# All elementwise products and sums of tiles on VectorE instead of GpSimd

## The chip, the cores and the metric

The kernel runs on one core of a Trainium2 chip. A core has five engines that run their own instruction streams side by side: TensorE (matrix products; PE in the profile, with the loading of its weights shown apart as PEld), VectorE (DVE), ScalarE (ACT), GpSimd (POOL) and SyncE (SP), which here issues all the transfers between the chip's memory (HBM) and the core's memory (SBUF). Matrix products land in a small memory of their own, PSUM. Instructions of different engines wait for each other by semaphores; within one engine they run in the order in which they were issued.

The metric is the time of one execution on the device in microseconds (us), and of several executions the median.

## The reference, cut to what matters

The program is a stack of four layers over 2048 tokens of width 1024, all in 32-bit floating point, with a batch of one. Each layer has the same frame, and its own mixing inside:

```python
h   = x @ w_in                      # 1024 -> 2560 to 4360 columns
mix = ...                           # the layer's own mixing of h, width 1024
out = mix @ w_out                   # 1024 -> 1024
x   = layer_norm(alpha * x + out)   # layers 1 to 3
x   = x + out                       # layer 4, whose input is normed by rms_norm
```

The mixings: layer 1, a gated linear recurrence (chunked) beside sliding-window attention with rotary positions; layer 2, gated linear attention beside a spatial gating unit with a norm of its own; layer 3, retention with rotary positions beside a pooling over 2, 4, 8 and 16 tokens; layer 4, banded attention, a matrix memory with gates (mLSTM) and a depthwise convolution of width 31 with a norm. Nearly every part ends in a gate, such as

```python
o = o * silu(hg)                    # layer 1; the same form in layers 2 to 4
```

so elementwise products of tiles are everywhere, and that is what the change is about.

## The kernel before, in words

**Tiling.** The 2048 tokens are cut into four blocks of 512. A stage is one layer on one block. `run` goes through them in the order: layers 1, 2, 3, 4 for blocks 0 and 1 (layer 1 block 0, layer 1 block 1, layer 2 block 0, and so on), then the same for blocks 2 and 3: 16 stages. In a stage the 512 tokens are either four row tiles of 128 tokens (tokens on the partitions), or column tiles of 128 features by 512 tokens.

**Products in three parts.** Full precision of the large products is reached by splitting each operand in a high and a low part: `ah` and `al` for the activations, `hi` and `lo` (both in one buffer `whl`) for the weights, and three matmuls each, hi x hi, lo x hi and hi x lo. `weight` (from L439) loads a weight tile into `wst` (two buffers), casts it on ScalarE to the high part (L450) and subtracts on VectorE for the low part (L315 by way of `tt`). The pair is written to HBM (`wdr`, L454) and from the second block on it is only loaded (L446). `whl` has four buffers. So the first stage of each layer converts all its weights, and the other three load them.

**One stage.** `load_x` loads the transposed rows that the layer before has stored and splits them into `ah` and `al`. Then come the input projections: `in_b` and `in_b4` (features on the partitions; `in_b4` uses four weight tiles twice, for 256 tokens each), and `in_a` (tokens on the partitions). Between them stands the layer's mixing, whose result is kept in `mix`. Its parts are transposed and split again (`split_mix`, or `split_ch` where they are already in column tiles), and `out_proj` forms the output in two halves of 512 columns. It adds the residual (`big<-big,acc` in the profile), takes the mean and variance (`bn_stats`, `rstd1`), and norms. For the odd row tiles two VectorE instructions per half norm and scale at once (`big<-big,mv,u` and `big<-big,vy,u`). For the even row tiles ScalarE norms and the scaling is left to `tail`. The single-column instructions of `rstd1` are named `ve`, `vy`, `vh`, `vf` and `vt`; they form an inverse square root step by step, each from the one before.

**The tails.** `tail` (from L650) belongs to a finished stage, but is traced in the input projections of the next one: `out_proj` puts four calls in a list, and `in_b4` takes one after each of its first groups (`flush`). It transposes a row tile for the next layer, stores the transposed tile (`chn`, L670) and, for the even row tiles, scales and shifts the row tile in place with `lng` and `lnb` (two halves, a product and a sum each), then stores the row tile for the residual of the next layer (`rows`, L676). These stores, and the loads of weights, are all in SP's queue.

**What sets the order.** The kernel does not write out the order of instructions of an engine. A planner (the tile framework's scheduler) goes through the traced instructions with a model of their durations and issues on each engine what is ready and comes first by priority. Priority is the order of tracing, except in `with self.hp():`, which moves instructions 2500 places ahead (weights and gates are traced so), and `self.later(2000)`, which moves them back (the 62 instructions of the wide convolution). The framework also sets the waits.

**What runs on GpSimd before the change.** All of it by `tt` (from L314) with an engine given. In every stage of layers 1 to 3 `tail`; in `gate_mix` and in layer 1 the gates (`mix<-mix,g`, `mix<-mix,u`); in `split_ch` and layer 4 the low parts of channels of `mix` (`al<-mix,ah`); in layer 2 the scale and shift of the spatial unit's norm and its gate; in layer 3 two of three steps of the rotation and the first step of the pooling; in layer 4 a scaling before the convolution, the scale and shift of the norm behind it, the squares and the scaling of the head norm, the division in `ml_head` and two gates. Beside these GpSimd has only memsets, selects and four copies.

## Time and profile before

| | |
|---|---|
| median of 3 runs | 3770.92 us |
| lowest and highest | 3770.17 and 3778.20 us |
| the profiled execution, its own time | 3774.09 us |
| its span in the profile | 3772.3 us |
| mean granted clock of TensorE | 0.995 |
| TensorE busy | 97% |
| VectorE busy | 58% |
| ScalarE busy | 37% |
| GpSimd busy | 14% |

How to read the rows: a group gives line, engine, operation, output<-inputs by the program's names, shapes and the count, then its busy time in us and the mean of one in ns, then the idle time of the engine just before them and what ended it. A row of the waits gives who waited for whom, the total in us, how often, and the longest. A row of the timeline begins with the start in us and the length; where the engine stood idle before it, the idle time and its releaser stand in brackets. A row of the windows gives the stretch and its length, the busy time and count of PE, PEld, DVE, ACT and POOL, then TensorE's granted clock (1.00 is full speed), the share of the transfer engines in use and GB/s. Most vector operations have line 315, 312 or 321, the lines of the helpers `tt`, `stt` and `ts`, so that the names of the tiles tell them apart. Recorded durations of two VectorE instructions in a row can overlap by some 0.1 us.

### The profile page before, as it was taken

Reading aid. Unit: us, or ns where it says so; the run is one execution under the profiler, and the core shown is the slowest. Engines: PE = TensorE matmul, PEld = TensorE weight load, DVE = VectorE, ACT = ScalarE, POOL = GpSimd, SP = SyncE. Lnnn points to the kernel's source line nnn. Section 1 sums busy time; section 2 is a strip of 40 time slices with the busy share of each in tenths; the row PEclk is TensorE's granted clock in tenths of the full one; section 3 lists DMA queues with packets and bytes.
Section 4 is the critical chain, followed back from the end, with each engine's and each line's share of the span. In section 5 each row is a group of like instructions: output and inputs, shape, how many; then the busy total and the mean of one; then the engine's idle time right before and its main releaser. Section 6 shows DMA issues by size and latency. Waiting matters only on the chain.

```text
span 3772.3 us, 53592 instructions
## 1 busy us (share of the span) xinstructions
PE 3677.3 (97%) x20576; PEld 3100.4 (82%) x20576; DVE 2177.9 (58%) x5387; ACT 1384.2 (37%) x2889; POOL 542.1 (14%) x445
## 2 busy tenths in 40 slices
PE   7999999999999999999999999999999999999999
PEld 6788888887888888788888878888887878888887
DVE  6765556555655598577456455443544545872873
ACT  5636343323241354325254263312221313441441
POOL 0020111112121200300200201111121311011002
PEclk9999999999999999999999999999999999999999
DMA  6775567855886576752544645747565756435434
GB/s 229 261 263 177 187 239 273 311 199 195 300 304 215 213 260 223 261 197 101 208 179 164 226 152 187 255 161 256 185 231 206 253 193 246 146 140 209 177 123 157
DMA packets 161680, 798.04 MB, mean 212 GB/s; under 512 B 17936, under 2 KB 18064, under 8 KB 93840
## 3 DMA queue, kind: packets, MB, share of 16 engines
q1 hardware_dynamic: 161424, 794.62, 58.4%
q8 instruction: 162, 2.65, 0.3%
q14 instruction: 94, 0.77, 0.1%
HBM read 593.02 MB, written 201.52 MB: 211 GB/s over the span
## 4 chain that ended last, share of the span: by engine, by line
PE 49%; DVE 6%; DMA 2%; ACT 2%; issue 1%; POOL 0%; SPq 0%; DVEq 0%; POOLq 0%; ACTq 0%
PE acc L324 41%; PE mm L324 6%; PE mm L327 3%; DVE u L312 2%; DMA whl<-wdr 1%; DVE t L315 1%; ACT t L301 0%; DVE big L312 0%; DMA wst<-in_wo_dram 0%; DVE t L1034 0%; DVE ss L1400 0%; ACT u L301 0%; POOL mix L315 0%; DVE mix L312 0%; ACT u L1424 0%
## 5 line engine op out<-in xcount | busy, mean ns | idle before, releaser
L324 PE MATMUL acc<-whl,ah 128*128 128x512 f32 (+3 forms) x6144 | 1816.2, 380 | 15.1 <-DVE whl L315 4.1
L324 PEld LDWEIGHTS acc<-whl,ah 128*128 128x128 f32 x6144 | 1112.0, 188 | 242.9 <-issue 7.1
L324 PE MATMUL acc<-whl,al 128*128 128x512 f32 (+3 forms) x3072 | 1156.8, 377 | 0.0
L324 PE MATMUL acc<-ah,whl 128*128 128x256 f32 (+1 forms) x4096 | 1076.8, 346 | 46.0 <-DVE whl L315 17.3
L324 PEld LDWEIGHTS acc<-ah,whl 128*128 128x128 f32 x4096 | 707.1, 191 | 135.0 <-DVE whl L315 18.6
L324 PE MATMUL acc<-al,whl 128*128 128x512 f32 (+1 forms) x2048 | 699.2, 342 | 0.5 <-DVE al L315 0.2
L324 PEld LDWEIGHTS acc<-whl,al 128*128 128x128 f32 x3072 | 578.0, 188 | 114.0
L324 PEld LDWEIGHTS acc<-al,whl 128*128 128x128 f32 x2048 | 391.5, 191 | 40.5 <-issue 2.9
L315 DVE TENSOR_TENSOR whl<-wst,whl 128x1024 fp32r<-128x1024 f32 (+2 forms) x140 | 173.3, 1244 | 142.0 <-ACT whl L450 131.5
L315 POOL TENSOR_TENSOR big<-big,u 128x512 f32<-128x512 f32 x96 | 139.1, 1471 | 562.0 <-PE mm L327 421.6
L450 ACT CAST whl<-wst 128x1024 fp32r<-128x1024 f32 (+2 forms) x140 | 143.3, 1027 | 149.3 <-DMA wst<-in_wi_dram 76.1
L548 ACT CAST ah<-u 128x512 fp32r<-128x512 f32 x128 | 79.3, 619 | 307.0 <-PE acc L324 200.1
L312 DVE SCALAR_TENSOR_TENSOR g<-g,acc 128x512 f32<-128x512 f32 x80 | 54.6, 686 | 204.3 <-ACT g L301 204.2
L312 DVE SCALAR_TENSOR_TENSOR u<-mix,hdw,u 128x512 f32<-128x512 f32 x240 | 165.6, 742 | 0.1
L315 POOL TENSOR_TENSOR mix<-mix,g 128x512 f32<-128x512 f32 x56 | 77.4, 1385 | 592.2 <-DVE g L312 574.2
L312 DVE SCALAR_TENSOR_TENSOR big<-big,acc 128x512 f32<-128x512 f32 x128 | 86.7, 684 | 120.2 <-PE acc L324 118.5
L301 ACT ACTIVATE g<-acc 128x512 f32<-128x512 f32 x72 | 42.6, 596 | 232.0 <-PE acc L324 226.4
L301 ACT ACTIVATE t<-mm,cols 128x128 f32<-128x128 f32 (+2 forms) x272 | 99.6, 463 | 66.6 <-PE mm L327 62.7
L315 POOL TENSOR_TENSOR u<-u,lc 128x512 f32<-128x512 f32 (+1 forms) x64 | 68.0, 1070 | 326.1 <-issue 170.0
L315 DVE TENSOR_TENSOR al<-u,ah 128x512 fp32r<-128x512 f32 x128 | 89.7, 702 | 42.1 <-ACT ah L548 41.0
L324 PE MATMUL mm<-big,u 128*128 128x256 f32 (+2 forms) x616 | 94.3, 289 | 7.3 <-ACT big L923 1.8
L324 PEld LDWEIGHTS mm<-big,u 128*128 128x128 f32 x616 | 84.3, 191 | 16.0 <-ACT u L1424 3.2
(342 smaller groups left out, 4376.8 us busy)
## 6 DMA issues: line engine op xcount, KB each, us to landing
whl<-wdr SPq DMA_DIRECT2D x396, 1024.0 KB, 4.8
wdr<-whl SPq DMA_DIRECT2D x132, 1024.0 KB, 5.3
wst<-in_wi_dram SPq DMA_DIRECT2D x100, 512.0 KB, 6.9
rows<-big SPq DMA_DIRECT2D x48, 512.0 KB, 4.0
chn<-t SPq DMA_DIRECT2D x96, 256.0 KB, 6.3
u<-chn SPq DMA_DIRECT2D x96, 256.0 KB, 6.6
big<-rows SPq DMA_DIRECT2D x48, 512.0 KB, 7.1
wst<-in_wo_dram SPq DMA_DIRECT2D x32, 512.0 KB, 6.0
```

The costliest lines, as they stand in the source:

```text
L301: return self.nc.scalar.activation(out, in_, f, bias=bias, scale=scale)
L312: return self.nc.vector.scalar_tensor_tensor(out, in0, s, in1, op0, op1)
L315: return (eng or self.nc.vector).tensor_tensor(out, a, b, op)
L324: return self.nc.tensor.matmul(out, lhsT, rhs, start=start, stop=stop)
L327: return self.nc.tensor.transpose(out, in_, self.ident)
L450: nc.scalar.copy(hi, st)
L548: nc.scalar.copy(h, c4(st))
```

## The change

Everywhere `tt` was given GpSimd as its engine, the argument is dropped, so VectorE runs the instruction. The instructions, their operands and their order in the program stay the same; memsets, selects and copies stay on GpSimd. The planner orders the engines' streams anew from the changed program.

```diff
 def split_ch(self, p, k):
-        self.tt(self.al[:, p], m, self.ah[:, p].bitcast(F32), ALU.subtract, self.nc.gpsimd)
+        self.tt(self.al[:, p], m, self.ah[:, p].bitcast(F32), ALU.subtract)
...
 def tail(...):
-                self.tt(xi, xi, lng[i], ALU.mult, nc.gpsimd)
-                self.tt(xi, xi, lnb[i], ALU.add, nc.gpsimd)
+                self.tt(xi, xi, lng[i], ALU.mult)
+                self.tt(xi, xi, lnb[i], ALU.add)
...
 def gate_mix(...):
-            self.tt(m, m, g, ALU.mult, self.nc.gpsimd)
+            self.tt(m, m, g, ALU.mult)
...
 def layer2(...):
-            self.tt(s, s, sg, ALU.mult, nc.gpsimd)
-            self.tt(s, s, sb, ALU.add, nc.gpsimd)
+            self.tt(s, s, sg, ALU.mult)
+            self.tt(s, s, sb, ALU.add)
...
-            self.tt(us[t], us[t], g, ALU.mult, nc.gpsimd)
+            self.tt(us[t], us[t], g, ALU.mult)
...
 def layer3(...):
-            self.tt(sh, sh, S, ALU.mult, nc.gpsimd)
-            self.tt(s, s, sh, ALU.add, nc.gpsimd)
+            self.tt(sh, sh, S, ALU.mult)
+            self.tt(s, s, sh, ALU.add)
...
-                self.tt(cur[:, start:528], prev[:, start:528], prev[:, start - d:528 - d], ALU.add, nc.gpsimd if l == 0 else None)
+                self.tt(cur[:, start:528], prev[:, start:528], prev[:, start - d:528 - d], ALU.add)
...
 def layer4(...):
-            self.tt(x, x, cg_, ALU.mult, nc.gpsimd)
-            self.tt(x, x, cb_, ALU.add, nc.gpsimd)
+            self.tt(x, x, cg_, ALU.mult)
+            self.tt(x, x, cb_, ALU.add)
...
-            self.tt(ths[t], m, m, ALU.mult, nc.gpsimd)
+            self.tt(ths[t], m, m, ALU.mult)
...
```

The other lines are of the same form: the gates of layer 1 and layer 4, the scaling before the convolution, the scaling of the head norm, the low parts in layer 4's split and the division in `ml_head`.

More of the change, by code (lines that the diff above doesn't have):

```diff
@@ L881, in layer1 @@
             m = self.mix[:, c * 1024 + 512:c * 1024 + 1024]
-            self.tt(m, m, g, ALU.mult, nc.gpsimd)
+            self.tt(m, m, g, ALU.mult)
             for h in (c - 1, c, c + 1):
@@ L1361, in layer4 @@
                 self.stt(ub[i][:, 32:544], th, 1.0, ca[i], ALU.add, ALU.mult)
-            self.tt(ub[i][:, 32:544], ub[i][:, 32:544], RS, ALU.mult, nc.gpsimd)
+            self.tt(ub[i][:, 32:544], ub[i][:, 32:544], RS, ALU.mult)
             nc.vector.tensor_copy(ub[i][:, 0:32], self.ch[:, i])
@@ L1469, in layer4 @@
             m = self.bandv(c)
-            self.tt(m, m, halves(g), ALU.mult, nc.gpsimd)
+            self.tt(m, m, halves(g), ALU.mult)
         mv, v = self.s(8, "mv8"), self.s(4, "v4")
@@ L1514, in layer4 @@
             m = self.mix[:, t * 1024 + 256:t * 1024 + 768]
-            self.tt(c4(m), c4(m), y[:, 4 * t:4 * t + 4].unsqueeze(2).to_broadcast([128, 4, 128]), ALU.mult, nc.gpsimd)
+            self.tt(c4(m), c4(m), y[:, 4 * t:4 * t + 4].unsqueeze(2).to_broadcast([128, 4, 128]), ALU.mult)
         def split(p):
@@ L1521, in split @@
                 nc.scalar.copy(halves(self.ah[:, p]), m)
-                self.tt(halves(self.al[:, p]), m, halves(self.ah[:, p].bitcast(F32)), ALU.subtract, nc.gpsimd)
+                self.tt(halves(self.al[:, p]), m, halves(self.ah[:, p].bitcast(F32)), ALU.subtract)
             else:
@@ L1752, in ml_head @@
         dst = self.mix.rearrange("p (t c) -> p t c", t=4)[:, :, 256 + h * 128:384 + h * 128]
-        self.tt(dst, nums[:, :, 0:128], d.unsqueeze(2).to_broadcast([128, 4, 128]), ALU.mult, nc.gpsimd)
+        self.tt(dst, nums[:, :, 0:128], d.unsqueeze(2).to_broadcast([128, 4, 128]), ALU.mult)
     def run(self):
```

## The prediction

> **What bounds the kernel now.** I read the page first, then the waits of TensorE, then the stages, then the places where TensorE stood longest. The busy times:
>
> ```profile
> PE 3677.3 (97%) x20576; PEld 3100.4 (82%) x20576; DVE 2177.9 (58%) x5387; ACT 1384.2 (37%) x2889; POOL 542.1 (14%) x445
> ```
>
> TensorE is busy for 97% of the span; 95 us are left in which it could be made to wait less. GpSimd is far from a bound, and VectorE has room on average. So the change is worth only what it does to the waits of TensorE, longest first:
>
> ```profile
> PE acc L324 <- DVE whl L315: 21.4, 8, 6.1
> PE acc L324 <- ACT whl L450: 10.8, 3, 10.0
> PE acc L324 <- ACT ah L548: 9.7, 3, 4.3
> PE acc L324 <- DMA whl<-wdr: 7.8, 9, 2.0
> ...
> PE acc L324 <- DVE g L312: 2.4, 2, 2.2
> ```
>
> No row of this list names POOL: TensorE never stood for a product made on GpSimd. The first row is the one that counts, and three waits make up nearly all of it. They stand at the start of the second, third and fourth layer in their first block. One of them, on the timeline:
>
> ```profile
> 508.14 10.85 POOL L315 TENSOR_TENSOR big<-big,u 128x512 f32<-128x512 f32 x8 [47.18 <-DVE nm L312]
> 508.37 1.61 DVE L312 SCALAR_TENSOR_TENSOR big<-big,mv,u 128x512 f32<-128x512 f32 x1
> ...
> 511.60 1.24 DVE L312 SCALAR_TENSOR_TENSOR vt<-vy,vh 128x1 f32<-128x1 f32 x1
> ...
> 512.88 1.21 DVE L312 SCALAR_TENSOR_TENSOR vy<-vt,vy 128x1 f32<-128x1 f32 x1
> ...
> 513.22 1.11 ACT L450 CAST whl<-wst 128x1024 fp32r<-128x1024 f32 x1
> ...
> 517.82 2.38 DVE L312 SCALAR_TENSOR_TENSOR big<-big,vy,u 128x512 f32<-128x512 f32 x2
> ...
> 520.12 2.35 DVE L315 TENSOR_TENSOR whl<-wst,whl 128x1024 fp32r<-128x1024 f32 x2
> ...
> 521.39 0.80 PE L324 MATMUL acc<-ah,whl 128*128 128x256 f32 x2 [5.57 <-DVE whl L315]
> ...
> 941.50 0.80 PE L324 MATMUL acc<-ah,whl 128*128 128x256 f32 x2 [5.23 <-DVE whl L315]
> ...
> 1307.07 0.80 PE L324 MATMUL acc<-ah,whl 128*128 128x256 f32 x2 [6.07 <-DVE whl L315]
> ```
>
> The cast half of the weight was there at 513.22 + 1.11 = 514.33, but VectorE made the other half (`whl`, L315) only at 520.12, since it was still in the layer norm of the stage before. Its instructions on a single column (`vt`, `vy`) took 1.2 us each, exactly as long as GpSimd was in its row of eight products. The same instructions at the end of another stage, while GpSimd was idle (groups by line, VectorE, 2380 to 2391 us):
>
> ```profile
> L312 DVE SCALAR_TENSOR_TENSOR big<-big,mv,u 128x512 f32<-128x512 f32 x2 | 1.5, 742 | 0.0
> L312 DVE SCALAR_TENSOR_TENSOR big<-big,vy,u 128x512 f32<-128x512 f32 x2 | 1.4, 750 | 0.0
> ...
> L312 DVE SCALAR_TENSOR_TENSOR vy<-vt,vy 128x1 f32<-128x1 f32 x4 | 0.6, 158 | 0.1
> ...
> L312 DVE SCALAR_TENSOR_TENSOR vt<-vy,vh 128x1 f32<-128x1 f32 x2 | 0.4, 216 | 0.0
> ```
>
> So an instruction of 158 ns took 1.21 us, and one of 742 ns took 1.61 us, beside a GpSimd product: the two engines take turns, and a VectorE instruction waits until the product under way is done. The long stall has a second price, in the windows just behind the three stalls:
>
> ```profile
> 523.00:525.00 2.00, 2.00 (x12) 2.00 (x11) 0.00 (x0) 0.00 (x0) 0.00 (x0) 0.50 1.01 422
> 525.00:527.00 2.00, 2.00 (x12) 2.00 (x12) 0.00 (x0) 0.00 (x0) 0.00 (x0) 0.58 1.12 360
> 527.00:529.00 2.00, 2.00 (x19) 2.00 (x18) 0.00 (x0) 0.00 (x0) 0.00 (x0) 1.00 0.84 260
> ...
> 945.00:947.00 2.00, 2.00 (x13) 2.00 (x12) 0.00 (x0) 0.00 (x0) 0.00 (x0) 0.62 1.07 373
> ...
> 1311.00:1313.00 2.00, 2.00 (x16) 2.00 (x15) 0.00 (x0) 0.00 (x0) 0.00 (x0) 0.81 1.05 315
> ```
>
> The sixth number after the length is the granted clock: 0.50 behind the stall, with 12 matmuls in 2 us where 19 run later. At 0.58 a window of 2 us holds 0.84 x 2 = 1.7 us of half clock, so it ends at 526.7; likewise at 946.5 and 1311.8.
>
> **The change, part by part.** Removed: every product, sum and difference of two tiles on GpSimd. The program keeps 37 others there (memsets, selects, four small copies), so 445 - 37 = 408 move, 32 of them 256 wide (eight in each layer 4 stage), the rest about 512. Added to VectorE: the same 408. The prices, and two rows of what VectorE loses now:
>
> ```profile
> L315 DVE TENSOR_TENSOR t<-t,lc 128x512 f32<-128x512 f32 x40 | 25.9, 688 | 0.5
> ...
> L315 DVE TENSOR_TENSOR t<-mm,t 128x256 fp32r<-128x256 f32 x8 | 3.3, 416 | 0.0
> ...
> L312 DVE SCALAR_TENSOR_TENSOR big<-big,mv,u 128x512 f32<-128x512 f32 x48 | 56.5, 1177 | 0.0
> ...
> L312 DVE SCALAR_TENSOR_TENSOR vt<-vy,vh 128x1 f32<-128x1 f32 x48 | 21.7, 453 | 0.0
> ```
>
> 376 x 0.688 + 32 x 0.416 = 272 us more work on VectorE. It gets back what it loses in turn-taking: 48 x (1177 - 742) ns = 21 us and 48 x (453 - 216) ns = 11 us in these two groups alone. Over all groups I estimate 150 us (the sum of each group's excess over its own undisturbed instances), bounded below by these 32. VectorE then stands at 2178 + 272 - 150 = 2300 us (61%), at worst at 2418 (64%). Both are far under TensorE, so this sum sets nothing; the places do.
>
> (1) The three layer starts. Between 508.3 and the weight VectorE has two `mv,u` (1.5 us), two `vy,u` (1.4) and about nine small ones (1.6): 4.5 us without turn-taking. Moved into its queue are the eight products of the two row tiles (`tail`), 5.5 us; four are ready at 508.1, the others only when TensorE has transposed the third row tile, at about 513. The weight is ready at 514.33 and is traced with a priority 2500 ahead, so the planner puts it before any product that has not been issued. With four products ahead: 508.4 + 4.5 + 2.8 = 515.7, and the weight is done 1.2 us later, at 516.9. TensorE wanted it at 521.39 - 5.57 = 515.8: a stall of 1.1 us in place of 5.6. If it goes as soon as the cast is there, at most one instruction late, it is done at 515.5 to 516.2: 0 to 0.4. I take 0.8. The bounds are 0 and 3.8 (all eight ahead: 508.4 + 4.5 + 5.5 + 1.2 = 519.6).
> Gain in stall: 5.57 + 5.23 + 6.07 - 3 x 0.8 = 14.5 us. Gain in clock: half of (526.7 - 521.4), (946.5 - 941.5) and (1311.8 - 1307.1), 2.6 + 2.5 + 2.3 = 7.5 us, if a stall of 0.8 leaves the clock alone. Together 22 us. A cross-check is the whole stages (cut behind the last residual sum of each):
>
> ```profile
> 505.00:719.00 214.00, 206.67 (x1197) 177.04 (x1197) 127.68 (x284) 81.62 (x149) 34.04 (x27) 0.98 0.77 287
> 719.00:925.00 206.00, 204.37 (x1202) 175.22 (x1201) 93.20 (x246) 59.41 (x126) 33.16 (x26) 1.00 0.59 213
> 925.00:1112.00 187.00, 180.06 (x960) 148.96 (x960) 120.58 (x274) 64.43 (x93) 37.06 (x28) 0.98 0.80 294
> 1112.00:1291.00 179.00, 178.42 (x970) 147.86 (x969) 87.28 (x238) 43.88 (x93) 38.17 (x28) 1.00 0.62 222
> 1291.00:1600.00 309.00, 291.35 (x1576) 243.10 (x1575) 239.08 (x503) 143.98 (x286) 48.58 (x40) 0.98 0.67 246
> ...
> 3160.00:3465.00 305.00, 300.17 (x1709) 254.87 (x1708) 202.13 (x475) 119.98 (x249) 45.02 (x40) 1.00 0.50 180
> ```
>
> The first block's stages of layers 2 and 3 are 8 us longer than the second's, which is stall plus clock (5.57 + 2.6, 5.23 + 2.5) and nothing else. So what is gained there isn't given back by the weight conversions behind it, which run in the same stages.
>
> [...]
>
> (2) The other consumers. Gates (56 products), splits (40), rope and pooling (48), spatial gate norm (32), layer 4's: on GpSimd they took 1.3 us in parallel, on VectorE 0.69 us in line. TensorE's wait list shows that their results have slack now. Behind each stands at most 0.69 us of delay for the next VectorE instruction; TensorE waits for VectorE some 50 times in all, mostly under 1 us, and each such wait can grow by one instruction or lose a turn of 1.2 us. Bounds: 50 x 0.69 = +35 us if each met one, -10 us if eight of them lost a turn. Few products fall into the dense stretches, so I take +2.
> (3) SP's queue issues the row stores (L676) behind the products of `tail`, and weight loads behind them:
>
> ```profile
> SPq L676 <- POOL big L315: 32.4, 21, 2.5
> ```
>
> That is 1.5 us a time; it would wait for VectorE instead, and the products take half as long there. 0, between -1 and +1 in each of 12 stages. ACT's and DVE's own waits for GpSimd go away; neither was on TensorE's path: 0.
> (4) Layer 4's end, the densest place for the moved work:
>
> ```profile
> 1500.00:1560.00 60.00, 55.68 (x254) 43.50 (x254) 42.38 (x93) 21.16 (x39) 30.49 (x25) 0.94 0.51 187
> ...
> 1800.00:1860.00 60.00, 59.25 (x288) 48.16 (x286) 31.77 (x77) 15.03 (x30) 25.93 (x25) 1.00 0.56 198
> ...
> 3360.00:3420.00 60.00, 59.20 (x291) 48.11 (x290) 33.38 (x86) 16.82 (x34) 24.44 (x24) 1.00 0.54 193
> 3660.00:3720.00 60.00, 58.90 (x295) 47.76 (x294) 33.28 (x82) 17.00 (x35) 21.89 (x22) 1.00 0.54 192
> ```
>
> Some 24 products in 60 us: 8 x 0.416 + 16 x 0.688 = 14 us onto a VectorE busy 42, 32, 33 and 33 us. It stays under 60 in all four, close only in the first. I take +2, all in the first.
> The planner orders each engine anew. Layers 2 and 3 repeat within 8 us, all of it explained above; I give it 0, and 8 us either way.
>
> Sum: profiled execution 3774.1 us (span 3772.3 and 1.8 around it) - 22 + 2 + 0 + 2 = 3756. The median of the runs, 3770.9, is 3.2 lower than that execution: **3753 us**.
>
> **The rivals.** (a) The same, with the products ahead of the weight: the stall stays 3.8 us, the clock falls as now, the gain is 5.6 - 3.8 = 1.8 us three times. 3774.1 - 5.4 + 4 = 3773, as a median 3769. For it: the order was made by a planner that put the weight behind the whole norm now. Against: the priority.
> (b) The layer starts get faster and the time is lost again at the weights' load, cast, split loop of the first block: 3771 + 0 to 3. Against it: the 8 us of the repeats.
> (c) Slower: the end of layer 4. There the norm of the convolution branch, the products for the head norm and the gates would queue between the cast weights and the splits on VectorE, and the output projection waits. It decides once VectorE is behind by more than the matmuls already released, about where 42 + 14 = 56 of 60 us stand now. Half of the 14 us late in four stages, with a half-clock stretch behind each as at the layer starts (2.5 us lost): 4 x (7 + 2.5) = 38 us, against a gain of 20: 3774 - 20 + 38 = 3792, as a median 3789. For it: the stage at 1291 has VectorE busy for 239 of 309 us. Against it: the other three ends have 27 us free.
> [...]
>
> **How the numbers follow.** About 0.2% (7.5 us) is what this kernel's measurement can tell from no change. Forecast 0.55, (a) 0.15, (b) 0.10, (c) 0.20. The forecast's own range is 3743 to 3766: nearly all faster (0.51), the rest the same. (a) gives 0.12 same and 0.03 faster, (b) 0.08 same and 0.02 slower, (c) 0.18 slower and 0.02 same. Sum: 0.54, 0.26, 0.20. The range goes from 3738 (no stall left at the layer starts, and 13 us of the bounds of 2 and the planner) to 3788, about (c).
>
> **What would show it.** In the profile of the changed kernel: 37 instructions on POOL; `vt` and `vy` at 0.2 us everywhere, `big<-big,mv,u` at about 0.74; TensorE's wait for `whl` L315 down from 21.4 to under 8 us; no clock of 0.50 behind the starts of layers 2 to 4; their first stages 6 to 8 us shorter. A wait for `whl` of 3 us or more at these three places makes (a) right; new waits of TensorE for `g`, `mix` or `al` behind the last input projection of layer 4 make (c) right. A VectorE that is not relieved (its long single-column instructions still there) would make the whole mechanism wrong.

## The result and the profile after

| | before | after |
|---|---|---|
| median of 4 runs each, taken together | 3773.11 us | 3725.51 us |
| lowest and highest | 3770.17 to 3778.20 us | 3723.16 to 3727.55 us |
| the profiled execution's own time | 3774.09 us | 3727.55 us |
| span in its profile | 3772.3 us | 3725.7 us |

The change makes the kernel faster by 47.6 us: a ratio of 0.9872, with an interval of 0.9855 to 0.9889. I had forecast 3753 us, a gain of 18, in a range that ended at 3738. The direction and the place of half of the gain were right; the other half was in terms that I had put at nothing or at a small loss.

The busy times, on the page of the kernel after:

```profile
PE 3665.1 (98%) x20576; PEld 3095.4 (83%) x20576; DVE 2267.0 (61%) x5795; ACT 1385.7 (37%) x2889; POOL 14.1 (0%) x37
```

GpSimd has its 37 instructions left, and VectorE stands at 61%. TensorE's waits, the longest groups of the kernel after (time in us, how often, the longest):

```profile
PE acc L324 <- ACT whl L450: 10.6, 3, 9.9
PE acc L324 <- ACT ah L548: 9.4, 3, 4.4
PE acc L324 <- DMA whl<-wdr: 8.4, 12, 1.3
PE mm L324 <- DVE u L312: 4.0, 8, 0.6
PE acc L324 <- DVE whl L315: 3.5, 4, 2.0
PE mm L327 <- DVE big L312: 3.3, 2, 1.7
```

The wait for `whl` of VectorE went from 21.4 us to 3.5, and the group for `g` is gone. The last group shown, for `big`, is new. The start of layer 2 in its first block, VectorE on the timeline of the kernel after:

```profile
506.62 0.74 DVE L312 SCALAR_TENSOR_TENSOR big<-big,mv,u 128x512 f32<-128x512 f32 x1
507.28 0.21 DVE L312 SCALAR_TENSOR_TENSOR vt<-vy,vh 128x1 f32<-128x1 f32 x1
...
508.02 0.15 DVE L312 SCALAR_TENSOR_TENSOR vy<-vt,vy 128x1 f32<-128x1 f32 x1
...
508.82 0.68 DVE L315 TENSOR_TENSOR big<-big,u 128x512 f32<-128x512 f32 x1
...
511.73 1.22 DVE L315 TENSOR_TENSOR whl<-wst,whl 128x1024 fp32r<-128x1024 f32 x1
```

The single-column instructions take 0.15 to 0.21 us, `mv,u` 0.74; the moved products (508.82 is one) stand between them and cost 0.68 each, and the low part of the weight is made at 511.73. TensorE's only idle time there is 0.22 us, for ScalarE's half of that weight. By stages (windows cut behind the last residual sum of a stage, as in the prediction):

```profile
502.00:708.00 206.00, 204.33 (x1197) 174.88 (x1196) 127.21 (x309) 81.65 (x149) 1.47 (x3) 1.00 0.81 298
...
914.00:1092.00 178.00, 177.18 (x959) 146.63 (x958) 123.62 (x302) 63.90 (x93) 0.00 (x0) 1.00 0.84 308
...
1270.00:1567.00 297.00, 288.28 (x1586) 243.70 (x1585) 242.85 (x546) 145.10 (x288) 1.05 (x2) 0.99 0.71 257
...
3120.00:3421.00 301.00, 299.58 (x1712) 255.25 (x1711) 212.47 (x515) 120.28 (x250) 1.05 (x2) 1.00 0.51 183
```

The first stage of layer 2 is 206 us long (214 before), that of layer 3 178 (187), that of layer 4 297 (309), and a later stage of layer 4 is 301 (305). The other two stages of layer 4 gain 3.9 and 2.6 us. So something is gained in every stage of layer 4, and in its first more than at its start.

### The profile page after: what moved, and what is told of

It reads as the page before. It is cut to its first block, busy times and chain, and to the rows that moved or that the text cites. A ratio compares the mean times of both kernels' runs of the same rounds, so it can differ in the third digit from the quotient of the medians.

```text
span 3725.7 us, 53281 instructions
## 1 busy us (share of the span) xinstructions
PE 3665.1 (98%) x20576; PEld 3095.4 (83%) x20576; DVE 2267.0 (61%) x5795; ACT 1385.7 (37%) x2889; POOL 14.1 (0%) x37
## 4 chain that ended last, share of the span: by engine, by line
PE 73%; DVE 7%; DMA 3%; ACT 2%; issue 1%; SPq 0%; POOL 0%; ACTq 0%; POOLq 0%; DVEq 0%
PE acc L324 61%; PE mm L324 8%; PE mm L327 3%; DMA whl<-wdr 2%; DVE u L312 1%; DVE big L312 1%; DMA wst<-in_wi_dram 1%; DVE t L315 1%; ACT t L301 0%; DVE whl L315 0%; DVE al L315 0%; DVE t L1034 0%; DVE ss L1400 0%; ACT u L301 0%; ACT whl L450 0%
## 5 line engine op out<-in xcount | busy, mean ns | idle before, releaser
L324 PEld LDWEIGHTS acc<-ah,whl 128*128 128x128 f32 x4096 | 700.4, 189 | 116.7 <-ACT ah L548 11.8
L312 DVE SCALAR_TENSOR_TENSOR big<-big,acc 128x512 f32<-128x512 f32 x128 | 86.8, 684 | 118.3 <-PE acc L324 116.5
L983 DVE CUSTOM_DVE_ANT_0 t<-mm,lc,nsk 128x256 f32<-128x256 f32 (+1 forms) x128 | 54.9, 472 | 49.8 <-PE mm L324 49.5
L324 PE MATMUL mm<-vb,t 128*64 128x128 f32 (+2 forms) x640 | 79.9, 280 | 2.8 <-DVE t L312 2.0
L324 PEld LDWEIGHTS mm<-vb,t 128*128 128x128 f32 (+1 forms) x640 | 68.4, 170 | 17.1 <-issue 11.4
```

Source lines behind the costliest of these rows:

```text
L312: return self.nc.vector.scalar_tensor_tensor(out, in0, s, in1, op0, op1)
L324: return self.nc.tensor.matmul(out, lhsT, rhs, start=start, stop=stop)
L983: nc.vector.tensor_tensor_reduce(out=p[:, o + off:o + 256], in0=ps[:, o + off:o + 256], in1=band[:, off:256], scale=-0.125, scalar=self.ns ...
```

## The experiments

Each time is a median, set against runs of the kernel before that were taken together with it on the same chip. In the first group products are moved in parts: `e1` and `e2` make up the whole, `e2` is `e3` and `e4`, `e3` is `e5` and `e6`, `e6` is `e13` and `e14`, and `e16` is a part of `e14`.

| moved to VectorE | products | median, us | before, us | difference | ratio and interval |
|---|---|---|---|---|---|
| all (the change) | 408 | 3725.51 | 3773.11 | -47.6 | 0.9872 (0.9855 to 0.9889) |
| `e1`: tails alone | 96 | 3748.21 | 3771.28 | -23.1 | 0.9939 (0.9926 to 0.9951) |
| `e2`: all but the tails | 312 | 3745.87 | 3771.28 | -25.4 | 0.9932 (0.9920 to 0.9945) |
| `e3`: layer 4 alone | 120 | 3752.31 | 3771.28 | -19.0 | 0.9948 (0.9936 to 0.9961) |
| `e4`: layers 1 to 3 without tails | 192 | 3766.66 | 3771.28 | -4.6 | 0.9986 (0.9977 to 0.9995) |
| `e5`: layer 4, scaling ahead of the convolution | 8 | 3763.10 | 3770.51 | -7.4 | 0.9983 (0.9974 to 0.9992) |
| `e6`: layer 4, the rest | 112 | 3754.32 | 3770.51 | -16.2 | 0.9961 (0.9947 to 0.9974) |
| `e13`: layer 4, squares, head scaling, splits | 40 | 3767.97 | 3771.34 | -3.4 | 0.9993 (0.9985 to 1.0002) |
| `e14`: layer 4, gates, norm, division | 72 | 3759.56 | 3771.34 | -11.8 | 0.9970 (0.9960 to 0.9980) |
| `e16`: layer 4, norm behind the convolution | 32 | 3766.81 | 3770.41 | -3.6 | 0.9988 (0.9979 to 0.9997) |

### The tails alone, and all but the tails

```diff
 def tail(...):
-                self.tt(xi, xi, lng[i], ALU.mult, nc.gpsimd)
-                self.tt(xi, xi, lnb[i], ALU.add, nc.gpsimd)
+                self.tt(xi, xi, lng[i], ALU.mult)
+                self.tt(xi, xi, lnb[i], ALU.add)
```

> Only the 96 products and sums of the tails (the scale and shift of two row tiles per stage, layers 1 to 3) move to VectorE; the other 312 stay on GpSimd. Theory T (turn-taking: a VectorE instruction with two tile operands or on a single column waits until the GpSimd product under way is done, and TensorE waits behind VectorE): the three long stalls at the first starts of layers 2, 3 and 4 go, with their half clock, -8 us each, and nothing else changes: -24 us, about 3749, first stages of layers 2 and 3 at 206 and 178 us, the first of layer 4 near 301, the half clock at the end of that stage still there. Theory P (the planner's new order of all engines made the gain): the stages change all over, and the sum is anywhere between -48 and +10.

Measured: -23.1 us. The first stages of layers 2, 3 and 4 are 7.9, 7.6 and 7.9 us shorter, and TensorE's wait for `whl` of VectorE is down to 4.9 us. This is the prediction's step 1 by itself. The other way about, with those two lines alone left on GpSimd:

```diff
 def tail(...):       # kernel after
-                self.tt(xi, xi, lng[i], ALU.mult)
-                self.tt(xi, xi, lnb[i], ALU.add)
+                self.tt(xi, xi, lng[i], ALU.mult, nc.gpsimd)
+                self.tt(xi, xi, lnb[i], ALU.add, nc.gpsimd)
```

> All products and sums move to VectorE but the 96 of the tails. Theory T: the three long stalls at layer starts stay at 5 to 6 us each with half clock behind them; the rest of the gain is there: -20 to -24 us, about 3750. Theory P: the layer starts are reshuffled too, so that the stalls are not what they were, and the sum with the run that moves the tails alone is far from the -48 us of the full change.

Measured: -25.4 us, with the stalls of the layer starts still there (stages of layers 2 and 3 within 1.5 us). The two parts make -48.5 us, the change -47.6; each part is uncertain by some 5 us, so within that they do not depend on each other. So half of the gain has nothing to do with the layer starts.

### Layer 4 alone, and layers 1 to 3 without the tails

```diff
 def layer4(...):     # the same with every product of layer 4; e4: with those of layers 1 to 3
-            self.tt(x, x, cg_, ALU.mult, nc.gpsimd)
-            self.tt(x, x, cb_, ALU.add, nc.gpsimd)
+            self.tt(x, x, cg_, ALU.mult)
+            self.tt(x, x, cb_, ALU.add)
```

> Only the 120 products of layer 4 move (30 in a stage: scaling before the convolution, its norm, head norm, division, gates, splits). Theory T: layer 4's four stages lose 5 us (beside the layer start, which stays), 4, 4.5 and 2.5 us, of which about 6 at the end of the first, where the 2.2 us wait for a gate and the half clock go: -14 to -17 us in all, about 3757. My prediction had these at +2 us (more load on VectorE): by it 3775.

> Only the 192 products of layers 1 to 3 outside the tails move (gates, splits, spatial norm, rotation, pooling). Theory T: almost none of TensorE's waits stand behind them: -3 to -6 us (layer 1's first and third stages), about 3769, the three layer starts as before. Theory L (products come sooner at their consumers, 0.7 in place of 1.3 us, and that is the gain): these are the most numerous products, and they should bring at least as much as the 120 of layer 4, -15 us or more.

Measured: -19.0 and -4.6 us. The second half sits in layer 4, in all four of its stages: -7.2, -4.0, -4.4 and -2.4 us in the profiled execution. A shorter way of each product through VectorE, wherever it stands, is not the reason: 192 such products in layers 1 to 3 bring 4.6 us.

### The scaling ahead of the convolution

Where in layer 4? The trace of before shows a place that I had not looked at, the start of its second stage. `mix<-mix,u` on GpSimd is the scaling ahead of the convolution (L1362); the timeline of before:

```profile
1624.64 1.29 POOL L315 TENSOR_TENSOR mix<-mix,u 128x512 f32<-128x512 f32 x1 [68.82 <-DVE mix L312]
1625.97 0.18 DVE L1364 COPY ch<-mix 128x32 f32<-128x32 f32 x1 [1.40 <-POOL mix L315]
...
1626.52 0.69 DVE L315 TENSOR_TENSOR t<-acc,u 128x512 f32<-128x512 f32 x1
...
1627.26 0.51 PE L324 MATMUL acc<-whl,ah 128*128 128x264 f32 x2 [0.68 <-DVE t L315]
```

VectorE stands 1.40 us at the copy `ch`, since it needs the scaled tile. In its queue behind that copy is `t<-acc,u`, which would empty an accumulator and could have run at once. TensorE waits for it, 0.68 us, and its row names `t` of VectorE, not GpSimd. The experiment moves that line alone:

```diff
-            self.tt(ub[i][:, 32:544], ub[i][:, 32:544], RS, ALU.mult, nc.gpsimd)
+            self.tt(ub[i][:, 32:544], ub[i][:, 32:544], RS, ALU.mult)
```

> Against the kernel before, only the scaling of the columns ahead of the convolution (L1362, two products in each of the four stages of layer 4, 8 in all) goes to VectorE; 400 products stay on GpSimd. Theory W (a queue of VectorE that stands): at the copy `ch` right behind the scaling VectorE waits 1.2 to 1.4 us for GpSimd, and TensorE behind it waits for the freeing product `t<-acc,u`; with the scaling on VectorE that wait is gone. The starts of the four layer 4 stages get 1.2 to 2.2 us shorter each, so 5 to 8 us faster (ratio about 0.998), at a load of 8 x 0.69 us on VectorE. Rival (the gain of layer 4 is the end of its first stage and the other three stages' turns, not this wait): 0, within 2 us. My prediction's own step 3 (VectorE's waits for GpSimd are not on TensorE's path) also says 0.

Measured: -7.4 us with 8 products of 408. The same place in its timeline:

```profile
1619.87 0.69 DVE L315 TENSOR_TENSOR mix<-mix,u 128x512 f32<-128x512 f32 x1
1620.59 0.18 DVE L1364 COPY ch<-mix 128x32 f32<-128x32 f32 x1
1620.69 0.69 DVE L315 TENSOR_TENSOR t<-acc,u 128x512 f32<-128x512 f32 x1
```

The copy follows without a wait, and the freeing product right behind it. The four stages of layer 4 are 2.4, 0.9, 2.4 and 1.9 us shorter. Theory W holds, at the upper end of what I expected. The -7.4 us is a net sum: the planner's new order for this run also has TensorE wait twice for `big` of VectorE in layer 4, 1.65 us each (1687.72 and 3546.03), where the kernel before has no such wait.

### The rest of layer 4

```diff
 def layer4(...):     # kernel before; only L1362 stays on GpSimd
-            self.tt(m, m, halves(g), ALU.mult, nc.gpsimd)
+            self.tt(m, m, halves(g), ALU.mult)
...                       # and L788, L1490, L1491, L1507, L1515, L1522, L1753 in the same way
```

> Against the kernel before, layer 4's other 112 products go to VectorE, and the scaling ahead of the convolution (8 products) stays on GpSimd. Theory W: together with the run that moves the scaling alone this makes up the -19 us that all 120 brought, so -11 to -14 us here: -7 in the end of layer 4's first stage (the wait for `g` and the half clock behind it) and about -1 to -2 in each other stage. Rival (the scaling is idle talk, the rest carries all): -19 us. Prediction's step 4 (more load on VectorE at the end of layer 4): +2 us. The start of the layer 4 stages shows the wait of `ch` for GpSimd unchanged.

Measured: -16.2 us, between the two theories: with the run before it the parts make -23.6 against the -19.0 of all 120. Each of these numbers is uncertain by 3 to 5 us, so the sum does not tell the two apart. 8.2 us of it are in layer 4's first stage. There TensorE had waited for `g` in the kernel before; I traced that back and took it first for VectorE's waits for the squares of the head norm, and moved these with the splits; a second run moves the others (L788, L1470, L1490, L1491, L1753):

```diff
-            self.tt(ths[t], m, m, ALU.mult, nc.gpsimd)
+            self.tt(ths[t], m, m, ALU.mult)
...                       # and the scaling (L1515) and low parts (L1522) in the same way
```

> Against the kernel before, of layer 4's products only those at the end of a stage go to VectorE: the squares for the head norm (L1507), its scaling (L1515) and the low parts of the split (L1522), 10 a stage, 40 in all. Theory Q (a chain over four queues in the end of layer 4's first stage): VectorE waits for GpSimd's squares, so it subtracts the low part of a weight late; SP's store of that weight pair waits for it, the load of the next weight stands behind the store, and two weights later TensorE waits 2.2 us for `g` and gets a half clock. Then this run alone brings the -6 to -8 us in that stage (block 0 of layer 4), no half clock behind 1550 us, and 0 to -1 in each of the other three: 7 to 10 us faster in all. Rival (the gates and the norm behind the convolution, which stand ahead of it, delay VectorE): that stage changes by less than 2 us here and by -6 to -8 in the run with the gates.

> Against the kernel before, the other 72 products of layer 4 go to VectorE: the gates (L788 for half tiles, L1470), the scale and shift behind the convolution (L1490, L1491) and the division in `ml_head` (L1753). The squares, the scaling of the head norm, the low parts of the split and the scaling ahead of the convolution stay on GpSimd. By theory Q the first stage's end keeps its wait for `g` and its half clock, or most of it, and the other turns bring about -1 us a stage: 2 to 6 us faster. By the rival 10 to 16 us faster, with the first stage 6 to 8 us shorter.

Measured: -3.4 us, an interval that holds no change, and -11.8. Layer 4's first stage is 2.1 us longer in the one and 5.5 shorter in the other. (The longer one has two stretches of half clock, 3.4 us each, at 1341 and 1379 us, behind waits of 1.52 and 1.89 us; the kernel before has the same waits, 1.52 and 1.88 us, and full clock behind them. Matmul by matmul the two stretches cost 3.1 us, so the stage got longer by them and not by the moved products.) Theory Q had the chain over the queues right, but not its beginning. In the timeline of before the chain begins on ScalarE (SPq is SP's queue of transfers):

```profile
1526.51 0.42 ACT L301 ACTIVATE u<-u 128x256 f32<-128x256 f32 x1 [2.66 <-POOL u L315]
...
1528.08 0.42 ACT L301 ACTIVATE u<-u 128x256 f32<-128x256 f32 x1 [1.15 <-POOL u L315]
...
1529.66 0.42 ACT L301 ACTIVATE u<-u 128x256 f32<-128x256 f32 x1 [1.16 <-POOL u L315]
...
1531.42 0.42 ACT L301 ACTIVATE u<-u 128x256 f32<-128x256 f32 x1 [1.35 <-POOL u L315]
...
1531.75 1.04 ACT L450 CAST whl<-wst 128x1024 fp32r<-128x1024 f32 x1
...
1535.46 4.56 SPq L454 DMA_DIRECT2D wdr<-whl  x2
...
1540.06 1.40 SPq L449 DMA_DIRECT2D wst<-in_wo_dram  x2
...
1545.88 1.05 ACT L450 CAST whl<-wst 128x1024 fp32r<-128x1024 f32 x1 [11.11 <-DMA wst<-in_wo_dram]
...
1549.76 0.73 PE L324 MATMUL acc<-whl,ah 128*128 128x512 f32 x2 [2.18 <-DVE g L312]
```

Read from the top: four activations of the norm behind the convolution wait for GpSimd's scale and shift, 6.3 us in all. The cast of a weight stands in ScalarE's queue behind them and begins only at 1531.75. The low part, the store of the pair (SP, 1535.46) and, behind that store in SP's queue, the next two loads (1540.06) are late in turn. ScalarE then waits 11.11 us for the load, and what empties the accumulators (`g`) stands behind that cast: TensorE waits 2.18 us. The queues of three engines lie between GpSimd and TensorE, and the wait of TensorE names only the last instruction of the chain. Behind it the clock falls; windows of before:

```profile
1550.00:1552.00 2.00, 1.76 (x6) 1.07 (x5) 2.00 (x3) 1.17 (x3) 2.00 (x2) 0.67 1.09 336
1552.00:1554.00 2.00, 1.73 (x5) 0.94 (x4) 1.41 (x3) 0.00 (x0) 2.00 (x2) 0.50 0.91 322
1554.00:1556.00 2.00, 2.00 (x6) 1.54 (x5) 0.30 (x1) 1.05 (x1) 1.82 (x2) 0.50 1.03 412
1556.00:1558.00 2.00, 2.00 (x7) 1.59 (x6) 0.92 (x1) 0.00 (x0) 0.00 (x0) 0.62 0.99 354
```

At a clock of 0.67, 0.50, 0.50 and 0.62 these 8 us lose 2 x (0.33 + 0.50 + 0.50 + 0.38) = 3.4 us. The next run moves the norm's scale and shift alone:

```diff
-            self.tt(x, x, cg_, ALU.mult, nc.gpsimd)
-            self.tt(x, x, cb_, ALU.add, nc.gpsimd)
+            self.tt(x, x, cg_, ALU.mult)
+            self.tt(x, x, cb_, ALU.add)
```

> Against the kernel before, only the scale and shift behind the convolution (L1490 and L1491, eight products of 128x256 in each stage of layer 4, 32 in all) go to VectorE. Theory R: in the end of layer 4's first stage ScalarE stands four times (2.66, 1.15, 1.16 and 1.35 us) for these products, and the casts of two weights stand in its queue behind them; the low parts, the stores of the pairs and the loads of the next weights follow late. Then the first stage gets 4 to 6 us shorter, as in the run with the 72 products, SP issues a load of `wo` there every 4 to 6 us instead of none between 1523 and 1540 us, and the whole is 4 to 8 us faster. Rival (the gates on GpSimd, or the division, are what holds the end): that stage within 2 us of before, and 0 to 3 us faster in all.

Measured: -3.6 us, a little under what theory R expected. In the profiled execution that stage is 4.2 us shorter, although it has the same two stretches of half clock (1343 and 1380 us) as the run with the squares. Matmul by matmul it gains 6.8 us from 1530 to 1560 us, where theory R had placed the gain, and loses 3.1 us at the two stretches. The timeline of this run, and one window behind it:

```profile
1537.41 2.10 SPq L449 DMA_DIRECT2D wst<-in_wo_dram  x2
...
1550.51 0.74 PE L324 MATMUL acc<-whl,ah 128*128 128x512 f32 x2 [0.33 <-DVE g L312]
```

```profile
1552.00:1554.00 2.00, 2.00 (x10) 1.58 (x9) 2.00 (x3) 0.00 (x0) 2.00 (x2) 1.00 1.02 248
```

The loads go out earlier, TensorE's wait for `g` is 0.33 us in place of 2.18, and the clock there stays at 1.00. That SP would issue a load every 4 to 6 us was wrong: two still go together, at 1537.41. The gates and the division make the rest of the 72 products' gain. One place of theirs, in the timeline of before:

```profile
1811.94 1.28 POOL L315 TENSOR_TENSOR mix<-mix,g 128x512 f32<-128x512 f32 x1 [0.63 <-DVE g L312]
1812.09 1.14 DVE L312 SCALAR_TENSOR_TENSOR d<-tb 128x4 f32<-128x4 f32 x1
...
1813.64 0.44 PE L327 MATMUL mm<-ident,u 128*128 128x128 f32 x2 [0.74 <-DVE d L315]
```

An instruction on four columns takes 1.14 us beside a gate on GpSimd, and TensorE waits for its result. Matmul by matmul, the run with the 72 products is 1.0 us earlier behind this place, and as much again behind the same place of both later stages; the run with the norm alone is not.

### GpSimd beside VectorE: products, and memsets

Is it the turn-taking of the two engines that made the layer starts slow, and not the order of the work? Both runs are the kernel after with extra work on GpSimd, whose results nobody reads; nothing is left out.

```diff
 def tail(...):      # kernel after, e7
                 self.tt(xi, xi, lnb[i], ALU.add)
+                for _ in range(2):
+                    nc.gpsimd.tensor_tensor(self.scr, xi, lng[i], ALU.mult)
```

> Against the kernel after, with nothing taken away: behind each scale and shift of a half row tile in the tail, GpSimd makes two extra products of 128x512 from the same tiles into a scratch tile that nobody reads (192 extra products if a tail has two halves and 12 stages two... each even row tile: 96 in all). No engine waits for their results. Theory T (turn-taking: a GpSimd product delays VectorE's single-column and scalar-tile instructions by up to a whole product): those instructions take about 1.2 us again at the starts of layers 2, 3 and 4, the stalls for `whl` return with 3 to 5 us and the half clock behind them, so 15 to 24 us slower than the kernel after, about 3745 us. Rival (the gain at the layer starts came from the order of the work or from the shorter way of the products, not from GpSimd running beside VectorE): no change, 3726 us, no stall over 1.5 us there.

Measured: 3736.88 us (3736.40 to 3742.40), 11.4 more than the kernel after, or 14.0 if each is set against its own runs of the kernel before. 96 extra products ran. Its timeline at the start of layer 2:

```profile
506.94 6.39 POOL L678 TENSOR_TENSOR scr<-big,u 128x512 f32<-128x512 f32 x4 [129.76 <-DVE vy L312]
507.29 1.25 DVE L312 SCALAR_TENSOR_TENSOR vt<-vy,vf 128x1 f32<-128x1 f32 x1
...
509.06 1.23 DVE L312 SCALAR_TENSOR_TENSOR vt<-vt 128x1 f32<-128x1 f32 x1
...
515.67 0.80 PE L324 MATMUL acc<-ah,whl 128*128 128x256 f32 x2 [4.02 <-DVE whl L315]
```

Products that nobody waits for bring the 1.2 us instructions and the stall of 4 us back (3.74 and 4.50 us at the starts of layers 3 and 4). The three first stages lose 5.6, 5.6 and 4.4 us of what they had gained, 15.6 together; the median shows 11.4 to 14.0, somewhat less than the 15 to 24 expected. The other run:

```diff
 def tail(...):      # kernel after, e8; scr of 128x256, tie of 4 columns
+                s = self.scr[t + i]
+                self.tt(self.tie[:, t + i:t + i + 1], xi[:, 0:1], s[:, 0:1], ALU.mult)
+                for _ in range(8):
+                    nc.gpsimd.memset(s, 0.0)
```

> Against the kernel after, at the same places as the run with extra GpSimd products: eight GpSimd memsets of 128x256 into scratch tiles (2.5 us together, about as long as two products), started behind the shift by a product of one column on VectorE. GpSimd writes as long as it did there, and reads nothing. If the turn-taking comes from GpSimd being busy at all or from its writes, `vt` and `vy` take as long as one memset (0.3 us and more) and the stalls come back in part: 5 to 20 us slower than the kernel after. [...]

Measured: 3688.22 us (3686.60 to 3689.11), 37 us less than the kernel after, which I had not expected. The next part shows that the memory set aside for it did this, not the memsets: without them, with the tiles at the same place, it is 3688.16. So 384 memsets cost nothing that can be measured. The timeline says the same:

```profile
506.65 4.58 POOL L683 MEMSET scr<- 128x256 f32 x16 [128.92 <-DVE tie L315]
507.11 0.15 DVE L312 SCALAR_TENSOR_TENSOR vt<-vt 128x1 f32<-128x1 f32 x1
...
507.30 0.15 DVE L312 SCALAR_TENSOR_TENSOR vy<-vt,vy 128x1 f32<-128x1 f32 x1
```

Beside a row of 16 memsets the single-column instructions take 0.15 us. So in these two runs GpSimd's products, which read tiles, delay VectorE (`vt<-vy,vf` takes 1.25 us), and its memsets, which only write, do not (0.15 us). That it is the reading that makes the difference, no run shows by itself. Nor is every instruction delayed beside a product: in the kernel before, `vy<-ve`, `vh<-ve` and `vf<-ve` (509.90 to 510.03), of one column each, took 0.14 us in the midst of GpSimd's eight products.

### The place of the tiles

In the run with the memsets each matmul of 512 columns was faster (one every 227 ns in place of 231 to 235). Its scratch tiles had moved all tiles behind them (`wst`, `whl` and the work tiles) by a multiple of 2048 bytes and 32 more. `ah` and `al`, the other operand, had stayed. Three runs do this to the kernels with no other work than one small memset at the start:

```diff
 def setup(...):      # e10: kernel after, e11: kernel before; 16 bytes, rounded up to 32
+        self.nc.gpsimd.memset(self.const([128, 4], F32, "pad"), 0.0)
         lb = self.const([128, 4], F32, "lb")
```

> Against the kernel after, one more tile of 16 bytes per partition is set aside (and set to zero once, at the start), which moves the weights (`wst`, `whl`) and all work tiles by 32 bytes, so that `whl` stands at 32 instead of 0 from a multiple of 64 bytes; `ah` and `al` stay where they are (32 from a multiple of 64). No instruction else. Theory A (place of the operands): the run with the memsets was 37 us faster than the kernel after since its scratch tiles moved `whl` in this way; a matmul of 512 columns there came every 227 ns instead of 232 to 235, one of 256 columns every 120 instead of 116.5. Then this kernel takes 3688 us, within 3. Rival (the memsets, or the order of the instructions, made that run faster): 3726 us, with a matmul of 512 columns every 232 to 235 ns.

> The kernel before with the same 16 bytes set aside and nothing else changed. Theory A with no part in the change: the gain is the same as in the kernel after, about -37 us, so 3734 us (3730 to 3738), and the difference between the two shifted kernels is again 45 to 48 us. If the place of the operands has a part in the turn-taking between VectorE and GpSimd, the difference between the shifted kernels is another by more than 5 us.

```diff
 def setup(...):      # e12: e10, and as many bytes ahead of ah
+        self.nc.gpsimd.memset(self.const([128, 4], F32, "pad0"), 0.0)
         self.ah = self.const([128, 8, TB], F32R, "ah")
```

> The kernel after with 16 bytes set aside ahead of `ah` and 16 bytes ahead of the weights: `ah`, `al`, `whl` and the work tiles all stand at a multiple of 64 bytes (and none but by chance at one of 2048). Tells apart two forms of theory A. If what counts is that the two operands of a matmul stand alike to a multiple of 64 bytes (both at 32 in the fast kernel, 32 and 0 in the slow), this is as fast as the run shifted by 32 bytes, 3688 us. If what counts is that `whl` stands off a multiple of 64 (or of 2048) by itself, it is 3726 us, or lies between for the one of 2048.

A fourth takes 64 bytes in place of 16:

```diff
 def setup(...):      # e15: kernel after
+        self.nc.gpsimd.memset(self.const([128, 16], F32, "pad"), 0.0)
         lb = self.const([128, 4], F32, "lb")
```

> The kernel after with 64 bytes set aside ahead of the weights, so that `whl` and the work tiles stand at a multiple of 64 bytes but at none of 2048 (84032 = 41 x 2048 + 64), while `ah` and `al` stay at 32 from a multiple of 64. If what made the shifted kernels fast is that both operands of a matmul stand alike to 64 bytes, this is as slow as the kernel after, 3726 us, with a matmul of 512 columns every 231 to 235 ns. If it is that `whl` leaves the multiples of 2048 bytes, it is as fast as they are, 3688 us, with 227 ns.

| bytes past a multiple of 64: `ah`, `whl` | kernel | median, us | ratio to before and interval |
|---|---|---|---|
| 32, 0 | after | 3725.51 | 0.9872 (0.9855 to 0.9889) |
| 32, 0 (`whl` off 2048) | `e15` | 3724.95 | 0.9878 (0.9865 to 0.9892) |
| 32, 32 | `e10` | 3688.16 | 0.9779 (0.9761 to 0.9797) |
| 0, 0 (`whl` off 2048) | `e12` | 3688.90 | 0.9781 (0.9766 to 0.9795) |
| 32, 32 | `e11`, kernel before | 3737.99 | 0.9911 (0.9894 to 0.9927) |

In these five, the three in which the two operands stand alike to a multiple of 64 bytes are 33 to 37 us faster than the same kernel without the shift; leaving the multiples of 2048 alone (`e15`) changes the median by 0.6 us, which is nothing that can be told from no change. Offsets other than 0 and 32 were not run. `e12` and `e15` have `whl` and all work tiles at the same addresses and differ by the 32 bytes ahead of `ah`. The groups of matmuls by shape, first of the kernel after, then of `e10`, then of `e15` (count, busy time, mean ns of one):

```profile
L324 PE MATMUL acc<-whl,ah 128*128 128x512 f32 x5120 | 1627.1, 398 | 4.8 <-DVE whl L315 2.9 <-DVE mix L312 1.5 <-DMA whl<-wdr 0.3
L324 PE MATMUL acc<-whl,al 128*128 128x512 f32 x2560 | 1011.9, 396 | 0.0
```

```profile
L324 PE MATMUL acc<-whl,ah 128*128 128x512 f32 x5120 | 1598.5, 393 | 5.2 <-DVE whl L315 2.8 <-DMA whl<-wdr 1.5 <-DVE mix L312 0.8
L324 PE MATMUL acc<-whl,al 128*128 128x512 f32 x2560 | 997.8, 391 | 0.0
```

```profile
L324 PE MATMUL acc<-whl,ah 128*128 128x512 f32 x5120 | 1624.2, 398 | 4.0 <-DVE whl L315 2.9 <-DVE mix L312 0.8 <-DMA whl<-wdr 0.2
```

Each is 5 ns shorter in `e10`, and by the starts of successive matmuls in the trace they follow each other every 227 ns in place of 231 to 235; over some 10,750 matmuls of this width 5 ns are 54 us, of which matmuls of 256 columns (every 120 ns in place of 116.5) take a part back. The effect has no part in the change: both kernels stand alike before and after it, and shifted kernel against shifted kernel it is 3737.99 - 3688.16 = 49.8 us, against 47.6. `e10` beats both kernels, by 2.2% the one before and by 1.0% the one after.

### The price of the load

```diff
 # kernel after, e9: behind each of the 408 products, and behind 24 more
+        self.again(a, b)        # nc.vector.tensor_tensor(scratch, a, b, ALU.mult)
```

> Against the kernel after, behind each of the 408 moved products VectorE makes a second one of the same size from the same tiles into a scratch tile that nobody reads; this is extra work, nothing is taken away. The scratch tile is 4096 bytes per partition, so the tiles behind it keep their place to a multiple of 2048 bytes. VectorE's load rises by another 272 us, from 61% to about 68%, in the same places where the change put its own 272 us. My prediction priced the first 272 us at +4 (2 for the other consumers, 2 for the end of layer 4): this should cost 0 to +10 us against 3725.5, so at most 3736. Rival (c) of the prediction, the end of layer 4 as VectorE's bound: +38 us or more, the waits of TensorE for `g`, `mix` or `al` in the ends of layer 4's stages, and a step like it in the kernel after would then be hidden in its gain.

The doubled line of the pooling in layer 3 also makes 24 sums that were on VectorE before the change, so 432 instructions are added and not 408 (6227 - 5795 in the rows). Measured: 3733.38 us (3732.76 to 3735.97), 7.9 more than the kernel after, or 9.8 if each is set against its own runs of the kernel before. Its busy times, and one of TensorE's waits:

```profile
PE 3664.3 (98%) x20576; PEld 3092.8 (83%) x20576; DVE 2506.6 (67%) x6227; ACT 1386.5 (37%) x2889; POOL 14.1 (0%) x37
```

```profile
PE mm L337 <- DVE mix L315: 4.4, 2, 3.9
```

VectorE takes on another 240 us, and 8 to 10 of them reach TensorE. They do so at one place: layer 4's first stage is 7.3 us longer than in the kernel after, and no other stage is longer by more than 1.5. At the end of that stage, at 1536.93, TensorE waits 3.92 us for `mix`, and 6.8 us of half clock follow. This is the place and the wait that rival (c) named, at twice the load that it was named for. In the kernel after TensorE does not wait there: between 1482 and 1568 us its profile shows no wait of TensorE over 0.15 us. What the first 408 products cost by themselves this run does not show; it shows that the next 432 cost no more than 10 us.

## Why the prediction was wrong, step by step

**(1) The layer starts: right.** Forecast -22 us; the run with the tails alone brings -23.1. Matmul by matmul the kernel after is 8.0, 7.8 and 8.0 us earlier behind the three starts, 23.8 in all. The mechanism was turn-taking, as the run with extra products shows (1.25 us for a single-column instruction beside them). In the trace of before, five single-column instructions in a row (511.60 to 517.78) each end at most 0.02 us behind the end of a GpSimd product. The low part of the weight was made at 511.73, 0.4 us behind the cast with one product between, and the longest stall left at the three starts is 0.48 us (at 923.57) and not 0.8. Rival (a), products ahead of the weight, did not come about, though the planner did put five products ahead of that weight, in between the steps of the norm. The clock of the two first stages of layers 2 and 3 is 1.00 in the rows above (0.98 before).

**(3) "ACT's and DVE's own waits for GpSimd go away; neither was on TensorE's path: 0": this is the step that failed.** Both kinds of wait lead to TensorE, through the queue of the engine that waits. VectorE's wait at `ch` holds the product that frees an accumulator (-7.4 us alone). ScalarE's waits for the norm behind the convolution hold two weight casts, and by way of SP's queue the next loads (-3.6 alone). SP's queue, which I also put at 0, is a link of that chain. These waits were in the trace of before; the rows for ScalarE and for VectorE:

```profile
ACT u L301 <- POOL u L315: 44.0, 16, 8.9
```

```profile
DVE ch L1364 <- POOL mix L315: 6.4, 5, 1.4
```

I had set them aside since TensorE's own list "names no POOL". That list names the last releaser alone, and at both places here the last releaser (`t` at 1627.26, `g` at 1549.76) is an innocent instruction that stood in its queue behind a waiting one. To rule such a wait out, the next instructions in that queue have to be looked up, and who needs them.

**(2) and (4) The other consumers and layer 4's end: the wrong sign.** Forecast +2 and +2; measured -4.6 in layers 1 to 3 and -19.0 in layer 4. The +4 as the price of VectorE's load alone is not contradicted: a second load of that size costs 8 to 10 us. What was mis-sized is the relief: I had put at most -10 us on it ("if eight of them lost a turn"), and priced turn-taking at the three long stalls only. Short waits, of 0.7 us at the start of layer 4's stages and at the division, and one of 2.2 us at the end of its first stage, made as much again. A price there was, and it is in the -19.0: in two stages of layer 4 TensorE now waits for `big`, 1.66 and 1.65 us, as in the run with the scaling alone; and in the first it waits 2.02 us for `t` at 1459.28, where it waited 1.01 before, as in the run with the 72 products. Rival (c), slower at the end of layer 4, expected the reverse of what happened there: the weights' work was late since GpSimd was slow, not since VectorE was full. By the run with the load doubled, VectorE would be what ends that stage if it had to take on as much again.

**VectorE's load: near, with one term too large.** Forecast 2300 us, measured 2267. The doubled load adds 240 us for 432 instructions, 0.555 us each, so the 408 cost some 226 us and not 272: recorded durations overlap (by 0.08 us at 1620.69 in the run with the scaling alone), and a sum of means counts the overlaps twice. The turn-taking then gave back 2178 + 226 - 2267 = 137 us, against an estimate of 150.

**The planner and rival (b).** The parts moved separately add up to the whole within what these runs can tell (-23.1 and -25.4), so no large gain comes from the new order by itself, and the gain of the layer starts was not lost later. Its small effects are the new waits for `big`.

What stays open: of the 72 products with the gates, the norm alone brings 3.6 of 11.8 us. Some 1 us a stage of the remainder is shown at the division, in three of the four stages; the rest I have not traced. And the parts of layer 4 add up to -22.6 (`e5`, `e13`, `e14`) where all of them bring -19.0, within what these runs can tell.

## What to carry to other kernels

A wait of an off-path engine is free only if nothing behind it in that engine's queue feeds the path: follow each wait one queue further before it is put at nothing (here 7.4 and 3.6 us hung on two such places). A product on GpSimd can cost more than its own time: beside one, `vy<-vt,vy` on VectorE took 1.21 us here in place of 0.16, and `big<-big,mv,u` 1.61 in place of 0.74. Before work is moved to relieve an engine, measure what it does to the other engine from its new place.

## What the hardware showed that I had not expected

**The place of a matmul's operands.** 32 bytes of memory set aside are worth 37 us here, 1.0%, four fifths of what the change brings: TensorE's pace for wide products (one every 227 ns, or every 231 to 235) went, in the five placings of the table, by whether both operands stand alike to a multiple of 64 bytes. Why, no run here shows.

**The clock falls after short stalls, and not each time.** A wait of 2.18 us (before, 1549.76) was followed by 6.8 us of half clock, in the run with the squares one of 1.99 us by 3.4 us, and in the run with the gates one of 1.46 us by none. In the kernel after, waits of 1.53, 2.02 and 1.65 us (1312.28, 1459.28 and 3513.33) were followed by 3.4 us each, and waits of 2.01 and 1.66 us (1350.64 and 1658.86) by none. With the extra products on GpSimd, stalls of 4.02 and 3.74 us cost 3.4 us of half clock each, one of 4.50 us cost 6.8. So the length of the wait alone does not decide it here: 1.53 us was followed by a fall, and 2.01 us was not. The kernel before also shows such a stretch at 2186 us in its profile, in a stage of layer 1, where the waits just ahead of it are 1.0 us and shorter. The profiles of five kernels with that stage unchanged (`e3`, `e5`, `e6`, `e13`, `e14`) do not have it, and the stage is 4 to 5 us shorter in them; the kernel after has it, at 2145 us. One profiled execution can hold a few us that are no part of a comparison.
